# A hybrid encoder block on one core: narrower score and value products, and new due times for a planned order

## The chip, the cores and the metric

The kernel runs on one core of a Trainium2 chip, as one launch. The metric is device time in microseconds (us); it was 699.15 us before the change, the median of three runs (699.06 to 699.29). The engines go by the names of the profile: PE is TensorE (matrix products), PEld is its loading of stationary operands, DVE is VectorE, ACT is ScalarE, POOL is GpSimd, SP is SyncE, which here only issues DMAs.

## The reference

One block over 512 tokens of width 1024, all in float32. Cut to what matters:

```
hn = rms_norm(h, ln_mix)
q1,q2,k1,k2,va, qf,kf,vf,fg, qc,kc,vc = split(hn @ w_in)      # 3590 columns
# three groups of heads, 64 wide: A (4, two score maps each), B (6), C (6)
s  = q @ k.T * scale + bias          # bias: ALiBi / forget gate / relative position
pr = softmax(where(allowed, s, -1e30))    # A: pr1 - lam * pr2
o  = pr @ v                          # A: rms_norm per head behind it
h  = h + concat(o_a, o_b, o_c) @ w_out
h  = h + conv_gated_mlp(rms_norm(h), w_up, conv_w, conv_b, w_down)   # 2816 wide
h  = h + (p @ w_ple_proj) * sigmoid(rms_norm(h) @ w_ple_gate)
```

A query sees keys of its own and earlier chunks of 64 only (B: of its own and earlier positions), so a block of 128 queries needs scores against the key blocks up to its own: 128, 256, 384 and 512 keys for the four query blocks.

## The kernel before, in words

Tokens lie in four blocks of 128. Every weight product is done in float32r (the reduced float32 that PE takes) as three products, high by high, high by low and low by high, so that float32 accuracy is kept; a weight tile is loaded (SP), cast to its high part (ACT, `whi`) and subtracted to its low part (DVE or POOL, `wlo`). One PE instruction multiplies a stationary operand of 128 by 128 with a moving operand of 128 rows by up to 512 columns, into one of eight PSUM banks: `z` (2), `s` (2), `t` (3), `o` (1).

The first 280 us or so hold the input projection (steps in1_0 to in9_3, three products each of a token block, up to 384 columns) with the attention of the heads laid between. For a head the steps are: `qk_cols` (PE transposes of `zn` into a `t` bank, then `q`, `k` and the low part `kl`), `scores`, `prob_cols`, `values`. `softmax_map` does a query block's scores as two products into an `s` bank, `k` and `kl` against `q`; DVE adds the bias and finds the maximum (`e`, `st`), ACT takes exp. Its width is `N = max(L, 256)`: the first query block needs L = 128 columns and computes 256. There are 20 such maps (16 heads, A has two each), and 16 heads in `values`, where four key blocks are accumulated into the `o` bank. Each is a high and a low product (`pth` and `ptl` for key blocks 0 and 1, `ptc` for 2 and 3); key block 3 concerns 128 queries only, but is moved as 256 columns whose first 128 are zeros (`off = min(kb, 2) * P`). The zeros are written once, by two ACT instructions at the start.

Behind that come the output projection, the gated MLP (22 blocks of the 2816 hidden columns, products of 256 and 512 columns) and the per-layer embedding, whose last steps are named gp.

The order of all instructions is set by a planner in the kernel itself (`Plan`). Every operation is recorded under the step's name, `due` gives PE operations a due time from their place in the written order plus a number of that step in the table `SHIFT`, and all other engines get theirs from the PE operation that needs them. `solve` then places the operations one by one on the engines by estimated durations, the earliest due first. `add` finds what an operation depends on from the regions that it reads and writes; only in the gp steps it takes a matmul as writing its whole bank.

Of the kernel before, what the change touches and what calls it, by code (L numbers as in the profile page):

```python
# [11 lines left out]
AF = mybir.ActivationFunctionType  # L12
# [3 lines left out]
P = 128  # L16
# [25 lines left out]
for _i in range(3):  # L42
# [8 lines left out]


SHIFT = {
# [41 lines left out]
}  # L95


# [29 lines left out]
class Plan:  # L127
# [26 lines left out]
    def add(self, eng, name, a, k):  # L154
# [4 lines left out]
        op.ready = 0.0  # L159
        for w, v in sorted(seen, key=lambda x: x[0]):  # L160
            r = self.region(v)
            if k.get("skip_group_check") and w and self.group.startswith("gp"):
                r = (0, P, 0, 4 * S)
            p0, p1, c0, c1 = r
            stand_in = STAND_INS.get(v.tensor.name)
            where = stand_in.place if stand_in and not stand_in.whole else v.tensor.name
            for other, _, _ in self.mem.get(stand_in.place, ()) if stand_in and stand_in.whole else ():
                if other.end is None:
                    op.deps.append(other)
            if where not in self.mem and v.tensor.space != bass.MemoryType.DRAM:  # L170
                op.ready = max(op.ready, self.fresh)
            log = self.mem.setdefault(where, [])
            for other, (q0, q1, d0, d1), t in self.there:
                if other == v.tensor.name and c0 < d1 and d0 < c1:
                    op.ready = max(op.ready, t)
            keep = []
            for rec in log:
                other, w2, (q0, q1, d0, d1) = rec
                hit = p0 < q1 and q0 < p1 and c0 < d1 and d0 < c1
                if hit and (w or w2) and other is not op:  # L180
                    if other.end is None:
                        op.deps.append(other)
                    elif not eng.name == other.eng.name == "pe":
                        op.ready = max(op.ready, other.end)
                if not (w and other is not op and p0 <= q0 and q1 <= p1 and c0 <= d0 and d1 <= c1):
                    keep.append(rec)
            keep.append((op, w, r))
            self.mem[where] = keep
# [137 lines left out]
def kernel(ctx: ExitStack, tc: tile.TileContext, x, xt0, xt, pt_in, small, g_ffn_in, bias_c,  # L326
# [266 lines left out]
    for b in range(2):  # L593
        for i in range(2):
            c = HALF[1 - i]
# [235 lines left out]


    ptc = [ap.tile([P, S], F32R, tag=f"ptc{b}", name=f"ptc{b}") for b in range(2)]
    for b in range(2):
        act.activation(ptc[b][:, 0:P], ident, AF.Copy, scale=0.0)

    def head_bias(kind, hd):

# [15 lines left out]

    def softmax_map(m, hh, qb, bias, rowb, name):
        L = (qb + 1) * P
        N = max(L, 256)
        q, k, kl = m[0][hh], m[1][hh], m[2]
        c = slice(qb * P, L)
        sp = bank("s", f"{name}_s")  # L860
        pe.matmul(sp[:, :N], q[:, c], k[:, :N], start=True, stop=False)
        pe.matmul(sp[:, :N], q[:, c], kl[hh][:, :N], start=False, stop=True)
        e = ap.tile([P, L], F32, tag=f"e{qb}", bufs=2, name=f"{name}_e")
        st = ap.tile([P, 4], F32, tag="st", bufs=12, name=f"{name}_st")
        init = 3.0e38
# [39 lines left out]
    def prob_cols(pr, hh):  # L905
# [20 lines left out]
        act.copy(th[:, P:], pt[:, P:])  # L926
        dve.tensor_tensor(out=tl[:, P:], in0=pt[:, P:], in1=f32(th[:, P:]), op=ALU.subtract)
        tiles.append((th[:, 2 * P :], tl[:, 2 * P :]))
        tiles.append((th[:, : 2 * P], tl[:, : 2 * P]))
        PT[pr, hh] = tiles  # L930
        yield

    def values(pr, hh):
# [5 lines left out]
        base = hh * HD  # L939
        po = bank("o", f"{pr}_{hh}_po")  # L940
        for kb in range(NT):
            off = min(kb, 2) * P
            v = V[pr][:, kb, hh * P : (hh + 1) * P]
            for j in range(2):
                pe.matmul(po[:, off:], v, PT[pr, hh][kb][j], start=kb == 0 and j == 0, stop=kb == 3 and j == 1)
# [1202 lines left out]
```

## Time and profile before

| what | us |
|---|---|
| median of three runs | 699.15 |
| profiled execution, from its first to its last instruction (span) | 697.6 |
| what lies around the span (median less span; the profiled execution's own time is not listed apart from it) | 1.55 |
| PE busy | 687.9 |
| DVE busy | 572.9 |
| ACT busy | 423.5 |
| POOL busy | 310.5 |

[...] A wait shows on PEld first: the load of the stationary operand is what carries the wait. From 20 to 640 us the granted clock of PE was 1.00 of full speed in every stretch.

### The profile page before, as it was taken

What the parts mean: (1) busy time and instruction counts of PE and PEld (TensorE: products, weight loads), DVE (VectorE), ACT (ScalarE), POOL (GpSimd) and SP (SyncE); (2) the same over time, 40 slices, a digit from 0 to 9 for tenths busy, and PEclk for the clock granted to TensorE, in tenths of its full rate; (3) what the DMA queues carried; (4) which work ended last, traced back from release to release, by engine and by line L of the source; (5) the groups of instructions that cost most, each with busy time, mean ns of one, the idle gap of its engine ahead of it and who ended that gap; (6) DMA issues with size and microseconds to landing.
All of it is one profiled execution on the core that took longest, in us unless ns stands there. A gap on an engine that the chain in (4) does not pass through costs nothing.

```text
span 697.6 us, 12855 instructions
## 1 busy us (share of the span) xinstructions
PE 687.9 (99%) x4600; PEld 643.3 (92%) x4600; DVE 572.9 (82%) x1159; ACT 423.5 (61%) x812; POOL 310.5 (45%) x418
## 2 busy tenths in 40 slices
PE   7999999999999999999999999999999999999997
PEld 7999999999999888899988999898998898999997
DVE  6688899888887873888996988789898899777867
ACT  6657676666675672766755544556536676446853
POOL 3677676756764661222231333421622502344561
PEclk9999999999999999999999999999999999999999
DMA  9543354413222152585865338764368654132433
GB/s 310 204 128 92 87 149 129 110 64 92 88 62 72 61 114 98 192 240 127 218 162 145 110 93 224 162 187 129 93 176 224 169 159 128 48 105 67 150 117 122
DMA packets 42989, 94.31 MB, mean 135 GB/s; under 512 B 4871, under 2 KB 9607, under 8 KB 42925
## 3 DMA queue, kind: packets, MB, share of 16 engines
q1 hardware_dynamic: 35868, 79.02, 35.8%
q0 software_dynamic: 6768, 14.16, 11.6%
q8 instruction: 36, 0.59, 0.4%
q10 hardware_dynamic: 288, 0.30, 0.1%
q14 instruction: 29, 0.23, 0.1%
HBM read 85.20 MB, written 4.21 MB: 128 GB/s over the span
## 4 chain that ended last, share of the span: by engine, by line
PE 96%; DVE 1%; POOL 1%; DMA 0%; ACT 0%; issue 0%; POOLq 0%
PE z L360 45%; PE s L360 23%; PE t L360 20%; PE o L360 8%; DMA zn<-in_w_in_dram 0%; DVE xh_again L360 0%; POOL rs L360 0%; POOL e L360 0%; DVE xl_again L360 0%; DVE kl L360 0%; DVE rs L360 0%; ACT xh_again L360 0%; POOL wlo L360 0%; DVE oall L360 0%; ACT sq L360 0%
## 5 line engine op out<-in xcount | busy, mean ns | idle before, releaser
L360 ACT CAST whi<-wraw 128x768 fp32r<-128x768 f32 (+2 forms) x146 | 108.4, 761 | 49.2 <-DMA wraw<-in_w_up_dram 10.6
L360 DVE TENSOR_TENSOR wlo<-wraw,whi 128x768 fp32r<-128x768 f32 (+2 forms) x128 | 112.8, 893 | 18.1 <-ACT whi L360 16.2
L360 PE MATMUL z<-whi,Th 128*128 128x384 f32 (+2 forms) x360 | 120.3, 346 | 4.8 <-ACT whi L360 4.6
L360 PE MATMUL z<-wlo,Th 128*128 128x384 f32 (+2 forms) x360 | 119.6, 342 | 0.0
L360 PE MATMUL z<-whi,Tl 128*128 128x384 f32 (+2 forms) x360 | 119.3, 341 | 0.0
L360 PEld LDWEIGHTS z<-whi,Th 128*128 128x128 f32 x360 | 67.8, 190 | 8.4 <-ACT whi L360 4.9
L360 PEld LDWEIGHTS z<-whi,Tl 128*128 128x128 f32 x360 | 67.8, 189 | 2.9
L360 PEld LDWEIGHTS z<-wlo,Th 128*128 128x128 f32 x360 | 68.1, 190 | 2.3
L360 POOL TENSOR_TENSOR wraw<-wraw,wraw 128x768 f32<-128x768 f32 (+2 forms) x21 | 28.1, 1343 | 82.7 <-DVE pin L360 41.0
L360 ACT ACTIVATE e<-e,st 128x128 f32<-128x128 f32 (+3 forms) x80 | 44.6, 559 | 16.6 <-DVE st L360 16.3
L360 PE MATMUL z<-Th,whi 128*128 128x256 f32 (+1 forms) x152 | 51.8, 341 | 0.0
L360 PE MATMUL z<-Tl,whi 128*128 128x256 f32 (+1 forms) x152 | 51.6, 340 | 0.0
L360 PE MATMUL z<-Th,wlo 128*128 128x256 f32 (+1 forms) x152 | 51.5, 340 | 0.0
L360 PE MATMUL s<-Tl,whi 128*128 128x256 f32 (+1 forms) x152 | 51.5, 340 | 0.0
L360 PE MATMUL s<-Th,wlo 128*128 128x256 f32 (+1 forms) x152 | 51.3, 340 | 0.0
L360 PE MATMUL s<-Th,whi 128*128 128x256 f32 (+1 forms) x152 | 51.1, 341 | 0.0
L360 POOL TENSOR_TENSOR rs<-rs,nhalf 128x4 f32<-128x4 f32 x40 | 43.2, 1090 | 4.9 <-DVE rs L360 1.4
L360 DVE CUSTOM_DVE_ANT_0 e<-s,bias 128x128 f32<-128x128 f32 (+3 forms) x74 | 33.9, 471 | 5.4 <-PE s L360 2.8
L360 POOL TENSOR_SCALAR e<-e,st 128x256 f32<-128x256 f32 (+3 forms) x48 | 29.1, 641 | 10.3 <-DVE st L360 8.3
L360 POOL DMA_DIRECT2D wraw<-in_w_up_dram x21 | 18.9, 902 | 31.4 <-DMA wraw<-in_w_up_dram 21.4
L360 PE MATMUL t<-whi,al 128*128 128x256 f32 x116 | 32.2, 282 | 0.0
L360 PE MATMUL t<-wlo,ah 128*128 128x256 f32 x116 | 32.1, 281 | 0.0
(342 smaller groups left out, 2286.6 us busy)
## 6 DMA issues: line engine op xcount, KB each, us to landing
wraw<-in_w_up_dram SPq DMA_DIRECT2D x41, 384.0 KB, 4.5
wraw<-in_w_in_dram SPq DMA_DIRECT2D x28, 384.0 KB, 3.6
wraw<-in_w_down_dram SPq DMA_DIRECT2D x17, 384.0 KB, 3.2
wlo_again<-in_w_up_dram SPq DMA_DIRECT2D x12, 384.0 KB, 4.3
whi_again<-in_w_up_dram SPq DMA_DIRECT2D x11, 384.0 KB, 4.5
wraw<-in_w_out_dram SPq DMA_DIRECT2D x16, 256.0 KB, 2.8
wraw<-in_w_up_dram SPq DMA_DIRECT2D x16, 256.0 KB, 3.9
wlo<-wraw POOLq DMA_DIRECT2D x7, 384.0 KB, 4.8
```

What stands on the lines that cost most here:

```text
L360: ins = getattr(self.eng, op)(*a, **k)
```

## The change

The scores of the first query block are computed 128 columns wide, the values of the last key block are moved 128 columns wide, and the two instructions that wrote the zeros are gone. In the planner, every PE instruction is taken as writing its whole bank. Of the numbers in `SHIFT` all but six are new, 20 steps that had none have one now, and one has lost it; of that table two lines stand here.

```diff
 SHIFT = {
-    "in1_1": 0.4, "in1_2": -4.5, "A0a": 0.1, "in1_3": -3.6, "in2_0": -0.9, "in2_1": 1, "A0b": 23.2, "in2_2": -4.2,
...
+    "in1_1": 0.6, "in1_2": -16.6, "A0a": 11.4, "in1_3": 2.9, "in2_0": 13.5, "in2_1": 16, "A0b": 24, "in2_2": 0.5,
...
@@ Plan.add
             r = self.region(v)
-            if k.get("skip_group_check") and w and self.group.startswith("gp"):
+            if w and eng.name == "pe":
                 r = (0, P, 0, 4 * S)
...
     ptc = [ap.tile([P, S], F32R, tag=f"ptc{b}", name=f"ptc{b}") for b in range(2)]
-    for b in range(2):
-        act.activation(ptc[b][:, 0:P], ident, AF.Copy, scale=0.0)
...
@@ softmax_map
         L = (qb + 1) * P
-        N = max(L, 256)
...
-        pe.matmul(sp[:, :N], q[:, c], k[:, :N], start=True, stop=False)
-        pe.matmul(sp[:, :N], q[:, c], kl[hh][:, :N], start=False, stop=True)
+        pe.matmul(sp[:, :L], q[:, c], k[:, :L], start=True, stop=False)
+        pe.matmul(sp[:, :L], q[:, c], kl[hh][:, :L], start=False, stop=True)
...
@@ prob_cols
-        tiles.append((th[:, : 2 * P], tl[:, : 2 * P]))
+        tiles.append((th[:, P : 2 * P], tl[:, P : 2 * P]))
...
@@ values
-            off = min(kb, 2) * P
+            off = kb * P
```

The program has 4,598 PE instructions before and after. 72 of them, which were 256 columns wide, are 128 now: 40 scores (20 maps, `k` and `kl`) and 32 values (16 heads, high and low). Apart from the two ACT instructions no other operation is added or removed, but nearly all of the program past the first 66 PE instructions stands in another order. Three places show it. In the rows, `s_130` and `s_131` are the two banks of scores, `t_146`, `t_149`, `t_150` those of transposes, `z_128` and `z_129` those of the projection, `o_148` the bank of values; a product reads moving operand, stationary operand; L360 and L363 are the same line of the helper that issues everything.

Place 1 is PE at the values of a head of A0, with the projection and transposes that stand between them. Before:

```order
L360 MATMUL z_129<-wlo_118,Th_64 128x256
L360 MATMUL o_148<-ptc_0_138,V_142 128x256
L360 MATMUL z_129<-whi_117,Tl_66 128x256
L360 MATMUL o_148<-ptc_0_137,V_142 128x256
L360 MATMUL z_129<-whi_120,Th_64 128x256
L360 MATMUL o_148<-ptc_0_138,V_142 128x256
L360 MATMUL z_129<-wlo_121,Th_64 128x256
```

And now, at the other head of A0:

```order
L363 MATMUL t_150<-ident,zn_91 128x128
L363 MATMUL o_148<-ptc_0_138,V_142 128x256
L363 MATMUL t_150<-ident,zn_91 128x128
L363 MATMUL o_148<-ptc_0_137,V_142 128x128
L363 MATMUL t_150<-ident,zn_91 128x128
L363 MATMUL o_148<-ptc_0_138,V_142 128x128
L363 MATMUL t_146<-ident,zn_91 128x128
L363 MATMUL z_129<-wlo_111,Th_64 128x384
```

The last two value products are 128 wide now, and here each is followed by a transpose; of the 72 narrow products 16 are followed by a transpose, 2 by another narrow one and 54 by a wider float32r product.

Place 2 is PE at the second score map of A0's first head. Before:

```order
L360 MATMUL t_149<-ident,bias_87 128x128 x3
L360 MATMUL s_130<-k_159,q_157 128x256
L360 MATMUL s_130<-kl_0_102,q_157 128x256
L360 MATMUL z_129<-whi_108,Th_64 128x384
L360 MATMUL z_129<-wlo_109,Th_64 128x384
L360 MATMUL z_129<-whi_108,Tl_66 128x384
L360 MATMUL z_129<-whi_108,Th_64 128x384
L360 MATMUL z_129<-wlo_109,Th_64 128x384
L360 MATMUL s_130<-k_159,q_157 128x384
L360 MATMUL s_130<-kl_0_102,q_157 128x384
```

And now:

```order
L363 MATMUL s_130<-k_159,q_157 128x128
L363 MATMUL z_128<-whi_114,Tl_67 128x384
L363 MATMUL s_130<-kl_0_102,q_157 128x128
L363 MATMUL t_149<-ident,bias_87 128x128 x4
L363 MATMUL s_130<-k_159,q_157 128x256
L363 MATMUL s_130<-kl_0_102,q_157 128x256
L363 MATMUL s_130<-k_159,q_157 128x384
L363 MATMUL s_130<-kl_0_102,q_157 128x384
L363 MATMUL z_129<-whi_108,Th_64 128x384
```

Before, five projection products stood between the scores of the second and of the third query block in bank `s_130`; now the third block's scores follow the second's in the same bank with nothing between.

Place 3 is PE at the first value product of A0's second head, which needs the cast `pth_181` of a bank of transposes. Before:

```order
L360 MATMUL t_149<-ident,e_0_95 128x128
L360 MATMUL z_129<-wlo_127,Th_65 128x256
L360 MATMUL t_149<-ident,e_0_95 128x128
L360 MATMUL z_129<-whi_126,Tl_67 128x256
L360 MATMUL z_129<-whi_126,Th_65 128x256
L360 MATMUL z_129<-wlo_127,Th_65 128x256
L360 MATMUL z_129<-whi_126,Tl_67 128x256
L360 MATMUL o_148<-pth_181,V_142 128x512
L360 MATMUL t_146<-ident,zn_91 128x128 x3
```

And now:

```order
L363 MATMUL t_146<-ident,e_0_95 128x128
L363 MATMUL z_128<-whi_114,Th_65 128x384
L363 MATMUL z_128<-wlo_115,Th_65 128x384
L363 MATMUL z_128<-whi_114,Tl_67 128x384
L363 MATMUL z_129<-whi_108,Th_64 128x384
L363 MATMUL z_129<-wlo_109,Th_64 128x384
L363 MATMUL z_129<-whi_108,Tl_66 128x384
L363 MATMUL o_148<-pth_181,V_142 128x512
L363 MATMUL t_149<-ident,zn_92 128x128
```

The value product stood four products of 256 columns behind the head's last transpose; now it stands six products of 384 columns behind it.

## Rows read from the trace of the kernel before

**Rows 1.** The page's parts 1 (busy time) and 4 (chain that ended last).
```profile
PE 687.9 (99%) x4600; PEld 643.3 (92%) x4600; DVE 572.9 (82%) x1159; ACT 423.5 (61%) x812; POOL 310.5 (45%) x418
...
PE 96%; DVE 1%; POOL 1%; DMA 0%; ACT 0%; issue 0%; POOLq 0%
```

**Rows 2.** Timeline, first 5 us: start, duration, engine, what, [idle before <-releaser].
```profile
2.95 0.51 ACT L360 ACTIVATE ptc<-ident 128x128 fp32r<-128x128 f32 x2
...
4.06 0.51 ACT L360 CAST whi<-zn 128x384 fp32r<-128x384 f32 x1 [0.60 <-DMA zn<-in_w_in_dram]
...
4.62 1.01 PE L360 MATMUL z<-whi,Th 128*128 128x384 f32 x2 [4.62 <-ACT whi L360]
```

**Rows 3.** Waits of PEld: who for whom, us in total, times, longest.
```profile
PEld z L360 <- ACT whi L360: 4.9, 2, 4.6
PEld s L360 <- DVE st L360: 0.9, 3, 0.4
PEld t L360 <- DVE zn L360: 0.6, 2, 0.4
...
PEld t L360 <- ACT pth L360: 0.4, 1, 0.4
...
PEld o L360 <- DVE ptl L360: 0.2, 1, 0.2
```

**Rows 4.** Groups by form: what, shape, count | busy, mean ns.
```profile
L360 PE MATMUL o<-ptc,V 128*128 128x256 f32 x64 | 17.0, 296 | 0.0
...
L360 PE MATMUL s<-k,q 128*128 128x256 f32 x40 | 11.4, 309 | 0.1
...
L360 PE MATMUL s<-kl,q 128*128 128x256 f32 x40 | 10.8, 298 | 0.0
```

**Rows 5.** Timeline of PE in two dense stretches, 512 and 256 columns.
```profile
109.63 0.39 PE L360 MATMUL s<-k,q 128*128 128x512 f32 x1
109.86 0.39 PE L360 MATMUL s<-kl,q 128*128 128x512 f32 x1
...
687.77 0.28 PE L360 MATMUL t<-whi,al 128*128 128x256 f32 x1
...
688.60 0.28 PE L360 MATMUL z<-whi,ah 128*128 128x256 f32 x1
```

**Rows 6.** Timeline of PE and PEld around a wait at 42.6 us.
```profile
42.65 0.19 PEld L360 LDWEIGHTS s<-k,q 128*128 128x128 f32 x1 [0.39 <-POOL k L360]
42.65 0.39 PE L360 MATMUL s<-k,q 128*128 128x256 f32 x1
...
42.76 0.19 PEld L360 LDWEIGHTS z<-wlo,Th 128*128 128x128 f32 x1
```

**Rows 7.** Transposes: the tile `e` (ns min/median/max), and two places of the timeline.
```profile
L360 PEld LDWEIGHTS t<-ident,e x160: 138/140/145, 56.3 to 265.7; 128*128 128x128 f32 x160
L360 PE MATMUL t<-ident,e x160: 270/272/328, 56.5 to 266.0; 128*128 128x128 f32 x160
...
116.19 0.93 PE L360 MATMUL t<-ident,e 128*128 128x128 f32 x7
...
132.34 0.20 PEld L360 LDWEIGHTS t<-ident,zn 128*128 128x128 f32 x2 [0.42 <-DVE zn L360]
```

**Rows 8.** The one float32 product: a place of the timeline, and its group.
```profile
88.18 1.02 PE L360 MATMUL o<-otmp,oall 128*128 128x512 f32 x2
...
L360 PE MATMUL o<-otmp,oall 128*128 128x512 f32 x4 | 2.0, 591 | 0.0
```

**Rows 9.** The wait of place 3, and DVE's reading of 256 columns of scores.
```profile
76.36 0.28 PE L360 MATMUL z<-whi,Tl 128*128 128x256 f32 x1
...
76.66 0.19 PEld L360 LDWEIGHTS o<-pth,V 128*128 128x128 f32 x1 [0.22 <-ACT pth L360]
76.66 0.50 PE L360 MATMUL o<-pth,V 128*128 128x512 f32 x1
...
L360 DVE CUSTOM_DVE_ANT_0 e<-s,bias 128x256 f32<-128x256 f32 x20 | 8.3, 420 | 0.7 <-PE s L360 0.4
```

83 rows, old and new, of the table SHIFT are left out of this document.

## The prediction

> **What bounds the kernel now.** I read the page first. PE is busy for 687.9 of 697.6 us, the next engine, DVE, for 572.9, and the chain that ended last is PE for 96% [rows 1]: the kernel is bound by what PE issues, and an engine off PE matters only where PE waits for it. The waits are therefore the second view. They stand on PEld: 17 rows, which add up to 10.6 us; 4.6 of that is the start, until the first cast weight arrives [rows 2, 3]. The remaining 6.0 us, single waits of 0.2 to 0.4 us for DVE, ACT and POOL, are the most that any new order of the program could win past the start; it is an upper end, because a load also counts as idle while the product before it still moves. The third view is the timeline of dense stretches, for the price of one product: two of 512 columns start 0.23 us apart, and seven distances of 256-column products take 0.83 us, 0.118 each [rows 5]. The mean durations of the groups that the change touches, 0.296 to 0.309 us [rows 4], are no price, since neighbours overlap.
>
> **The narrow products.** 72 products go from 256 to 128 columns: half of the 80 scores and half of the 64 values that rows 4 count at 256. Scaled by columns they would fall from 0.118 to about 0.06 us: the slope is (0.23 - 0.118)/256, so 128 columns are worth 0.056 us. But each product also needs its own stationary operand, and one place shows what that load takes when nothing covers it. At 42.65 us PE had waited for POOL, so the load of a score product lies bare: the product lasts 0.39 us instead of 0.28, and the next load starts 0.11 us after the first, just when the product begins to move [rows 5, 6]. So a float32r load takes 0.11 us, and the load for the following product begins only when the present one starts to move. Behind a 256-column product that load is covered (0.118 against 0.11). Behind a 128-column one it is not: the next float32r product can't start before 0.11 us. For 54 + 2 narrow products, which are followed by float32r, the saving is 0.118 - 0.11, some 0.008 us: 56 x 0.008 = 0.45 us.
>
> A transpose's load is shorter: two loads of 0.14 us take 0.20 together when they lie bare, so the second began 0.06 after the first [rows 7]. The 16 narrow products followed by a transpose, as at place 1, thus cost their own 0.06 us: 16 x 0.058 = 0.93 us. Together 1.4 us. The stage is PE's (it waits for little else), so I count it whole.
>
> For the ends: no float32r product under 256 columns stands in the trace. From below, all 72 at the column price win 72 x 0.058 = 4.2 us. From above, the nearest row of another rate is the plain float32 product, two records of 0.591 us that span 1.02, so 0.43 us apart and 0.86 for 512 columns [rows 8]; at that rate 128 columns take 0.215, and 72 x 0.097 = 7.0 us are lost. I take the load-bound price because it is nearest to what the rows show on the same kind of instruction; transposes, also 128 columns wide, are (0.93 - 0.27)/6 = 0.11 us apart [rows 7], which is the same sum.
>
> The bare load of rows 6 took 0.11 us, and that sets the sum above. [...]
>
> **The zeros.** The two ACT instructions lie at 2.95 to 3.46 us, and ACT then idles 0.60 us for the first weights' DMA [rows 2]. Removing them wins nothing; with that cover gone they would have cost 0.5 us.
>
> **The new order.** It can't add PE work (the count is unchanged), so it acts through waits alone. I weigh the places where they differ. At place 3 PE lost 0.3 us at 76.66: the value product started 0.30 us behind the one before it instead of 0.118, and lasted 0.50 instead of 0.39 since its load lay bare [rows 5, 9]. Added up with the spacings above, it stood 0.93 us of PE work behind the last transpose of the bank whose cast it needs, and now stands 1.16 us behind it. Over all heads, seven value products stood 1.05 us or less behind that transpose; now one does. PEld's waits for these casts and their low parts are four of its 17 rows, 0.4, 0.3, 0.2 and 0.2 us, of which rows 3 hold the first and the last; I count 0.8 of these 1.1 us as won. Late next is the low part from DVE, which stood behind the cast anyway. At place 2 the opposite happens: the third block's scores need the bank that DVE still has to read. The second block's last product ends 0.28 us after its start, DVE's read of 256 columns takes 0.42 [rows 9], and then the load lies bare for 0.11: 0.81 us instead of 0.118, so some 0.7 us are lost, and all of PE's queue behind it, the projection first, stands for so long. Two more score pairs (0.44 and 0.55 us behind the bank's last use, by the same count) may lose 0.1 to 0.2 us each. What the waits for `zn` and `st` become (1.5 us together, rows 3) can't be read from the order, since they hang on DVE's queue. That leaves gains and losses of about 1 us each that are known and, in the rest, up to some 3 us to be won, and hardly as much to be lost, as none of it is new work. The loads that SP and POOL issue move with their steps; past the start no row of PEld's waits names a DMA, so I count them at nothing, and a weight that came late would show as a wait for its cast `whi`, which is 0.3 us at most now. I take -0.5 us for the order, between -2.5 and +1.4. Taking whole banks as written changes no instruction; it only makes the planner keep products from a bank that another engine reads, and its effect is in this term.
>
> **Sum.** -1.4 - 0.5 = -1.9 us: a span of 695.7 instead of 697.6, and with the 1.55 us that lie between span and median, 697.2 us instead of 699.15 (-0.27%).
>
> **The rivals.** First, the loads hide after all and the narrow products run at column price: for it speaks that PEld is not busy all the time, against it rows 6 and the fixed order of one load ahead. -4.2 - 0.5 gives 694.4 us. [...] Second, the slower side: below 256 columns a float32r product falls back to the rate of plain float32. For it speaks that no such product was in the program and that a slower rate exists on this PE [rows 8]; against it that transposes of 128 columns, which are float32 too, take only 0.11 us. It decides from about 0.125 us per narrow product on (0.118, and the order's 0.5 us over 72); at full price it is +7.0 - 0.5, 705.6 us. Third, the narrow products go as forecast, but place 2 is typical of the new order and its waits give the gain back: +1.4 from waits makes 699.2 us. Fourth, that the change doesn't do what it says can be left out: the order of the changed program shows the 72 narrow products.
>
> **How the numbers follow.** Forecast 0.60, column price 0.07, float32's rate 0.13, waits give it back 0.20. About 0.2%, 1.4 us, is what a measurement of this kernel can tell from no change: faster means under 697.75, slower over 700.55. The forecast's own range is 695.2 to 699.2, by the order's ends; two thirds of it lie under 697.75. Faster: 0.60 x 0.68 + 0.07 = 0.48. Slower: 0.13 and a quarter of the third rival, 0.18. Same: the rest, 0.34. The range from 694.6 to 700.4 takes in the forecast, nearly all of the third rival and a little of the first, and leaves out the second.
>
> **What would show it.** In the profile of the changed kernel, a narrow score product followed by a projection product: the latter should start (or end) about 0.11 us later than a column-bound product would, with its load beginning at the narrow one's start; followed by a transpose, 0.06. At 0.06 throughout, the first rival holds, at 0.2 the second. At place 2 a wait of PEld for DVE's `st` of about 0.7 us, at place 3 none for `pth`. The sum of PEld's waits should stay at 5 to 6 us past the start; at 8 the third rival is true. Wrong would be the whole account if PE's idle time moved by several us at places where neither a narrow product nor a bank's reuse stands.

## The result, and the profile after

The changed kernel takes 702.35 us (median of four runs, 701.81 to 703.15) against 699.11 us of the kernel before on the same chip: a ratio of 1.0046, 95% interval 1.0031 to 1.006. It is slower by 0.46%. The forecast was 697.2 us, and its range ended at 700.4.

The page of the profiled execution (702.13 us, span 700.4), its parts 1 and 4, to be read against [rows 1]:

```profile
PE 686.6 (98%) x4600; PEld 642.4 (92%) x4600; DVE 574.8 (82%) x1159; ACT 425.9 (61%) x810; POOL 315.2 (45%) x418
...
PE 89%; POOL 3%; DMA 3%; DVE 2%; issue 1%; ACT 1%; POOLq 0%; ACTq 0%; DVEq 0%
```

PE is busy 1.3 us less than before and the span is 2.8 us longer. The chain, 96% PE before, now runs for 11% through other engines; POOL, 1% before, has 3%. So PE's work did not grow: PE stands still for longer. POOL's busy time has grown from 310.5 to 315.2 us with the same 418 instructions. That points at POOL.

The waits of PEld, all eleven rows (who waits for whom, us in total, times, longest), against [rows 3]:

```profile
PEld z L363 <- ACT whi L363: 4.6, 1, 4.6
PEld s L363 <- POOL k L363: 3.6, 4, 1.3
PEld s L363 <- DVE st L363: 1.6, 3, 0.7
PEld o L363 <- ACT otmp L363: 1.3, 1, 1.3
PEld z L363 <- issue: 1.0, 4, 0.2
PEld z L363 <- DVE conv L363: 0.9, 2, 0.6
PEld z L363 <- DVE Tl L363: 0.5, 1, 0.5
PEld o L363 <- issue: 0.5, 1, 0.5
PEld t L363 <- ACT whi L363: 0.3, 1, 0.3
PEld s L363 <- DVE wlo L363: 0.2, 1, 0.2
PEld t L363 <- DVE wlo L363: 0.2, 1, 0.2
```

Past the start they add up to 10.1 us instead of 6.0. The many small waits for `zn`, `pth` and `ptl` are gone; in their place stand four waits for `k` from POOL (3.6 us), three for `st` (1.6) and one for `otmp` (1.3). The same by another count, each PE instruction's distance end to end from the one before it less what such an instruction usually takes (0.118, 0.175 or 0.233 us for 256, 384 or 512 columns, 0.109 for a transpose, 0.43 for a float32 product), added up from 14 us on: PE lost 5.2 us before and 9.8 after.

The narrow products, one place of PE's timeline (start, duration) and PEld's beside it:

```profile
57.39 0.34 PE L363 MATMUL z<-whi,Th 128*128 128x384 f32 x1
57.56 0.22 PE L363 MATMUL s<-k,q 128*128 128x128 f32 x1
57.62 0.39 PE L363 MATMUL z<-wlo,Th 128*128 128x384 f32 x1
57.85 0.22 PE L363 MATMUL s<-kl,q 128*128 128x128 f32 x1
...
57.56 0.19 PEld L363 LDWEIGHTS z<-wlo,Th 128*128 128x128 f32 x1
57.67 0.19 PEld L363 LDWEIGHTS s<-kl,q 128*128 128x128 f32 x1
```

The product behind the narrow one starts 0.06 us after it, but lasts 0.39 instead of 0.34: its load began only at 57.56, with the narrow product, and took until 57.67, as the bare load of [rows 6] did. From the end of the first row to the end of the third are 0.28 us, of which 0.175 are the 384 columns; so the narrow product costs 0.11. Over all 54 such places a narrow product ends 0.06 behind the one before it, and its follower of 256, 384 or 512 columns ends 0.171, 0.227 or 0.285 behind the narrow product: together about 0.113 and the follower's own price. Before a transpose, narrow product and transpose together take 0.06 + 0.134 = 0.194, of which 0.109 are the transpose's: 0.085 for the narrow one.

Place 2, PE and DVE's reading of the second block's scores:

```profile
53.52 0.28 PE L363 MATMUL s<-kl,q 128*128 128x256 f32 x1
54.32 0.45 PE L363 MATMUL s<-k,q 128*128 128x384 f32 x1 [0.52 <-DVE st L363]
...
53.84 0.42 DVE L363 CUSTOM_DVE_ANT_0 e<-s,bias 128x256 f32<-128x256 f32 x1
```

The third block's scores start 0.80 us behind the second's, as forecast (0.81). Place 3's wait is gone.

Now the first trace of the cause in single instructions. POOL's copies of the low half of `q` and `k` (the helper `move`, 64x512), of which a head's scores need the last. The group of the tile `k`, ns min/median/max, after and then before:

```profile
L363 POOL TENSOR_SCALAR k<-k x30: 613/618/2027, 38.9 to 258.2; 64x512 fp32r<-64x512 f32 x30
```

```profile
L360 POOL TENSOR_SCALAR k<-k x30: 612/617/782, 38.2 to 247.0; 64x512 fp32r<-64x512 f32 x30
```

The same copy takes 0.61 us, or up to 2.03. Of all 60 copies ten take over 0.7 us (0.87 to 2.03), three before. Two places of the timeline of after, POOL and DVE, show what stands beside the long ones:

```profile
50.65 1.58 POOL L363 TENSOR_SCALAR k<-k 64x512 fp32r<-64x512 f32 x1
...
51.09 0.66 DVE L363 TENSOR_TENSOR wlo<-wraw,whi 128x512 fp32r<-128x512 f32 x1
...
52.28 0.33 PE L363 MATMUL s<-k,q 128*128 128x128 f32 x1 [0.58 <-POOL k L363]
...
156.79 1.87 POOL L363 TENSOR_TENSOR wlo<-wraw,whi 128x768 fp32r<-128x768 f32 x1 [0.23 <-ACT whi L363]
...
156.86 2.61 DVE L363 TENSOR_TENSOR wlo<-wraw,whi 128x768 fp32r<-128x768 f32 x1
...
160.56 0.69 DVE L363 TENSOR_TENSOR oall<-o,otmp 64x512 f32<-64x512 f32 x1
...
161.29 0.63 ACT L363 ACTIVATE otmp<-oall 128x512 f32<-128x512 f32 x1 [1.30 <-DVE oall L363]
...
161.97 1.13 PE L363 MATMUL o<-otmp,oall 128*128 128x512 f32 x2 [0.94 <-ACT otmp L363]
```

At 50.65 us a copy stands beside DVE's subtraction of two SBUF tiles and ends 0.48 us behind it; PE waits for that copy. All ten long copies stand beside such a subtraction for at least a part of their time (one of them, at 209.64 us, only for its last 0.19). At 156.86 it is the other way round: DVE's subtraction, 0.95 us by its median, takes 2.61 beside a subtraction of POOL's. DVE's queue is late by 1.7 us, with it `oall`, ACT's `otmp` and at last PE. The theory from here on: an instruction on POOL and a subtraction of two SBUF tiles on DVE that run side by side hinder each other, so that one of the two ends late. The rivals: narrow products that cost more than thought, waits that belong to the new order itself, or due times that only fit other rules.

### The profile page after: what moved, and what is told of

Read it like the earlier page. It is cut to its first block, busy times and chain, and to the rows that moved or that the text cites. A ratio compares the mean times of both kernels' runs of the same rounds, so it can differ in the third digit from the quotient of the medians.

```text
span 700.4 us, 12856 instructions
## 1 busy us (share of the span) xinstructions
PE 686.6 (98%) x4600; PEld 642.4 (92%) x4600; DVE 574.8 (82%) x1159; ACT 425.9 (61%) x810; POOL 315.2 (45%) x418
## 4 chain that ended last, share of the span: by engine, by line
PE 89%; POOL 3%; DMA 3%; DVE 2%; issue 1%; ACT 1%; POOLq 0%; ACTq 0%; DVEq 0%
PE z L363 41%; PE s L363 21%; PE t L363 19%; PE o L363 8%; DMA wraw<-in_w_up_dram 2%; POOL k L363 2%; POOL q L363 1%; DMA zn<-in_w_in_dram 0%; POOL wraw L363 0%; DVE conv L363 0%; POOL wlo_again L363 0%; ACT whi L363 0%; DVE wlo L363 0%; ACT otmp L363 0%; DVE xl_again L363 0%
## 5 line engine op out<-in xcount | busy, mean ns | idle before, releaser
L363 ACT CAST whi<-wraw 128x768 fp32r<-128x768 f32 (+2 forms) x146 | 109.4, 762 | 51.9 <-PE z L363 16.5
L363 DVE TENSOR_TENSOR wlo<-wraw,whi 128x768 fp32r<-128x768 f32 (+2 forms) x128 | 113.8, 901 | 17.3 <-ACT whi L363 16.3
L363 PE MATMUL z<-whi,Th 128*128 128x384 f32 (+2 forms) x360 | 123.1, 348 | 4.6 <-ACT whi L363 4.6
L363 PE MATMUL z<-whi,Tl 128*128 128x384 f32 (+2 forms) x360 | 122.9, 347 | 0.1
L363 PE MATMUL z<-wlo,Th 128*128 128x384 f32 (+2 forms) x360 | 122.5, 346 | 0.0
L363 PEld LDWEIGHTS z<-whi,Th 128*128 128x128 f32 x360 | 67.9, 189 | 7.9 <-ACT whi L363 4.6
L363 PEld LDWEIGHTS z<-whi,Tl 128*128 128x128 f32 x360 | 67.8, 189 | 3.8 <-DVE Tl L363 0.5
L363 PEld LDWEIGHTS z<-wlo,Th 128*128 128x128 f32 x360 | 67.8, 189 | 3.2
L363 POOL TENSOR_TENSOR wraw<-wraw,wraw 128x768 f32<-128x768 f32 (+2 forms) x21 | 29.7, 1416 | 66.9 <-DVE pin L363 25.9
L363 ACT ACTIVATE e<-e,st 128x128 f32<-128x128 f32 (+3 forms) x80 | 44.7, 560 | 23.7 <-DVE st L363 23.0
L363 PE MATMUL s<-Tl,whi 128*128 128x512 f32 (+1 forms) x152 | 51.9, 341 | 0.0
L363 PE MATMUL s<-Th,whi 128*128 128x256 f32 (+1 forms) x152 | 51.7, 342 | 0.0
L363 PE MATMUL s<-Th,wlo 128*128 128x256 f32 (+1 forms) x152 | 51.7, 341 | 0.0
L363 PE MATMUL z<-Th,wlo 128*128 128x256 f32 (+1 forms) x152 | 51.4, 340 | 0.0
L363 PE MATMUL z<-Tl,whi 128*128 128x256 f32 (+1 forms) x152 | 51.3, 340 | 0.0
L363 PE MATMUL z<-Th,whi 128*128 128x256 f32 (+1 forms) x152 | 51.2, 341 | 0.0
L363 POOL TENSOR_TENSOR rs<-rs,nhalf 128x4 f32<-128x4 f32 x40 | 42.3, 1060 | 5.4 <-DVE rs L363 2.9
L363 DVE CUSTOM_DVE_ANT_0 e<-s,bias 128x128 f32<-128x128 f32 (+3 forms) x74 | 34.0, 471 | 11.7 <-PE s L363 9.1
L363 POOL TENSOR_SCALAR e<-e,st 128x512 f32<-128x512 f32 (+3 forms) x48 | 28.4, 602 | 24.4 <-DVE st L363 19.4
L363 PE MATMUL t<-wlo,ah 128*128 128x256 f32 x116 | 32.7, 282 | 0.0
L363 PE MATMUL t<-whi,al 128*128 128x256 f32 x116 | 32.7, 282 | 0.0
L363 PE MATMUL t<-whi,ah 128*128 128x256 f32 x116 | 32.4, 282 | 0.0
```

The source lines that it names most:

```text
L363: ins = getattr(self.eng, op)(*a, **k)
```

## The experiments

**The two halves of the change apart.** First the 72 products at 128 columns in exactly the order of before, on every engine:

```diff
-        pe.matmul(sp[:, :N], q[:, c], k[:, :N], start=True, stop=False)
+        pe.matmul(sp[:, :N], q[:, c], k[:, :N], start=True, stop=False, swap=(sp[:, :L], q[:, c], k[:, :L]))
```

(`swap` holds the operands that are issued; the planner still sees the first ones. The values likewise; the zeros are still written.)

> The order of every engine is that of the kernel before, row for row; only the 72 products are 128 instead of 256 columns wide (the zeros are still written). Theory A (the loss comes from the new order; a narrow product saves little, because the next load isn't covered): in the trace after the change a narrow product and the float32r product behind it together end 0.005 us earlier than with 256 columns, with a transpose behind it 0.033 us earlier; here 61 have a product and 11 a transpose behind them, so -0.7 us: 698.4. Theory B (the narrow products themselves are what is slow, at float32's rate or by waits that they bring): +3 us or more. Theory C (column price, as the first rival had it): -4 us.

698.34 us (697.96 to 698.97), ratio 0.9992, interval 0.9983 to 1.0001: the narrow products win about 0.7 us, at the edge of what can be told.

Then the order of after with 256 columns, by the same device (the zeros are written at the start):

```diff
-        pe.matmul(sp[:, :L], q[:, c], k[:, :L], start=True, stop=False)
+        N = max(L, 256)
+        pe.matmul(sp[:, :L], q[:, c], k[:, :L], start=True, stop=False, swap=(sp[:, :N], q[:, c], k[:, :N]))
```

> The order of every engine is that of the changed kernel, row for row; only the 72 products are 256 columns wide again (and the zeros are written at the start, beside the first DMAs). Theory A: the loss stays, and the narrow products' 0.8 us are given back, in part into PE's waits: 702.4 to 703.2. Theory B: the loss goes, about 699.

702.6 us (702.28 to 703.01), ratio 1.0052 (1.004 to 1.0065). The loss is all in the order. PE's four waits for `k` stand in front of narrow score products in the changed kernel; with 256 columns the row is the same, so they do not come from the width:

```profile
PEld s L366 <- POOL k L366: 3.6, 4, 1.3
```

**The stretched copies on ACT.** After's order; the ten copies over 0.7 us are done by ACT at the same place of the program:

```diff
+                if len(MOVES) - 1 in ON_ACT:      # ten of the 60 copies
+                    return act.now("copy", a[:2], {}, pinned)
```

> The changed kernel in its own order, but the ten copies of q and k parts that POOL did in more than 0.7 us instead of 0.61 are done by ACT, at the same place of the order. Theory A1 (POOL's copies are stretched where DVE subtracts two SBUF operands beside them, and PE waits for the last copy of k: 0.8, 1.2, 0.4 and 0.6 us): PE's four waits for POOL go, -2.5 to -3 us, 699.5 us. Theory A2 (those copies stand too late in the order whoever does them): less than 1 us of change, 702.

699.39 us (698.68 to 701.35), ratio 1.0008 (1.0 to 1.0017): 3.0 us of the loss come back, and PE no longer waits for POOL's `k`. The copies that are left on POOL:

```profile
L370 POOL TENSOR_SCALAR k<-k x23: 611/617/625, 39.5 to 255.8; 64x512 fp32r<-64x512 f32 x23
...
L370 ACT CAST k<-k x7: 617/620/622, 51.5 to 256.7; 64x512 fp32r<-64x512 f32 x7
...
L370 POOL TENSOR_SCALAR q<-ql x19: 612/616/2007, 37.4 to 257.2; 64x512 fp32r<-64x512 f32 x19
```

The copies of `k` show no stretch any more. Four copies of `q` do (1.05 to 2.01 us): they now stand on POOL beside the DVE instructions where others stood. No row of PEld's waits names them: by this trace PE does not wait for them, and nothing shows that they cost time.

**The second collision.** On top of that, DVE's subtraction at 156.9 us goes six places back in DVE's queue, behind `oall` (with the refill of its raw tile, which SP issues):

```diff
+MOVED = [(1693, 1724), (1704, 1726)]   # place in the planned order, the place before which it is put
...
+            for a, b in MOVED:
+                order.remove(was[a])
+                order.insert(order.index(was[b]), was[a])
```

> The changed kernel's order with the ten stretched copies on ACT, and one more edit: DVE's subtraction wlo at 156.9 us, which stood beside POOL's subtraction and took 2.61 instead of 0.95 us, moves six places back in DVE's queue. Theory P (the wait of 1.2 us for otmp at 162 us comes from that stretch, since DVE's oall stands behind it): the wait goes, 699.4 - 1.2 = 698.2 us, between 697.9 and 698.6. Theory R (the wait belongs to the order: ACT and DVE come to otmp late anyway): 699.2 to 699.6 us, and PE still waits about 1.2 us at 162 us.

698.11 us (697.53 to 699.25, one outlier of 1125 us left aside), ratio 0.9988 (0.9978 to 0.9997). The timeline of DVE and PE:

```profile
158.36 0.56 DVE L382 TENSOR_TENSOR ptc<-t,ptc 128x384 fp32r<-128x384 f32 x1 [0.90 <-ACT ptc L382]
...
159.90 0.69 DVE L382 TENSOR_TENSOR oall<-o,otmp 64x512 f32<-64x512 f32 x1 [0.18 <-ACT otmp L382]
160.71 1.81 DVE L382 TENSOR_TENSOR wlo<-wraw,whi 128x768 fp32r<-128x768 f32 x2
...
161.38 1.07 PE L382 MATMUL o<-otmp,oall 128*128 128x512 f32 x2
```

PE no longer waits for `otmp` at this place, and the moved subtraction with the one behind it takes 1.81 us for both. The move takes the whole subtraction out of the queue ahead of `oall`, not the stretch alone. But DVE now stands idle for 0.90 us ahead of `ptc`, which waits for ACT: an unstretched subtraction of 0.95 us would have fitted there, so it is the stretch that made `oall` late. With these stretches out of PE's way the new order, 698.11 us, stands where the old one with the same narrow products does, 698.34. The two edits together bring back 702.35 - 698.11 = 4.2 us, which is all of the order's loss (702.35 - 698.34 = 4.0) within what can be told.

**The collision by itself.** Stages added behind the last step of the kernel before, each begun by an ACT instruction that writes what both engines read:

```diff
+    def copy(i):      # POOL, 64x512
+        pool.tensor_scalar(c[:64, i * 512 : i * 512 + 512], f32(a[:64, :512]), 1.0, 1.0, ALU.mult, ALU.mult)
+    def two(eng, t, i=0):      # two SBUF operands, 128x768
+        eng.tensor_tensor(out=t[:, i * 768 : i * 768 + 768], in0=f32(a[:, :768]), in1=f32(b[:, :768]), op=ALU.subtract)
+    def bank_read():      # one from PSUM, one from SBUF, 128x512
+        dve.tensor_tensor(out=d[:, :512], in0=bk, in1=f32(a[:, :512]), op=ALU.subtract)
```

> The program of before, with a row of small stages added behind its last step (so its time is some 40 us longer and not compared): in each, ACT writes an operand in SBUF and then POOL and DVE start on it together. Theory P (POOL and DVE hinder each other where both take two streams from SBUF): POOL's copy of 64x512 takes 0.61 us alone and beside DVE's subtraction that reads PSUM, but is stretched to 1.2 to 1.6 us beside DVE's subtraction of two SBUF operands (0.94 us) and to 2 us or more beside two such subtractions; DVE's subtraction, started after POOL's subtraction of 768 columns (1.87 us alone), takes 2.0 to 2.6 us instead of 0.94. Theory Q (the stretched copies come from something else of the changed program, as the many semaphores or the load of SBUF by all engines): the copy takes 0.6 to 0.7 us in every stage, and DVE's subtraction 0.94.

The timeline of POOL, then of DVE:

```profile
695.22 0.62 POOL L360 TENSOR_SCALAR Tl<-Th 64x512 fp32r<-64x512 f32 x1 [13.33 <-ACT Th L360]
...
702.12 1.80 POOL L360 TENSOR_TENSOR Tl<-Th,Th 128x768 fp32r<-128x768 f32 x1 [4.71 <-issue]
...
707.61 1.38 POOL L360 TENSOR_SCALAR Tl<-Th 64x512 fp32r<-64x512 f32 x1 [0.95 <-ACT Th L360]
...
712.26 0.61 POOL L360 TENSOR_SCALAR Tl<-Th 64x512 fp32r<-64x512 f32 x1 [0.94 <-ACT Th L360]
...
723.49 0.61 POOL L360 TENSOR_SCALAR Tl<-Th 64x512 fp32r<-64x512 f32 x1 [1.81 <-ACT Th L360]
...
726.78 1.80 POOL L360 TENSOR_TENSOR Tl<-Th,Th 128x768 fp32r<-128x768 f32 x1 [1.03 <-ACT Th L360]
...
734.00 1.80 POOL L360 TENSOR_TENSOR Tl<-Th,Th 128x768 fp32r<-128x768 f32 x1 [1.81 <-ACT Th L360]
```

```profile
698.30 0.96 DVE L360 TENSOR_TENSOR Tl<-Th,Th 128x768 fp32r<-128x768 f32 x1 [4.08 <-ACT Th L360]
...
707.55 0.96 DVE L360 TENSOR_TENSOR Tl<-Th,Th 128x768 fp32r<-128x768 f32 x1 [6.44 <-ACT Th L360]
...
712.42 1.26 DVE L360 TENSOR_TENSOR Tl<-Th,Th 128x768 fp32r<-128x768 f32 x1
...
723.44 0.69 DVE L360 TENSOR_TENSOR Tl<-t,Th 128x512 fp32r<-128x512 f32 x1 [0.95 <-ACT Th L360]
...
726.93 2.46 DVE L360 TENSOR_TENSOR Tl<-Th,Th 128x768 fp32r<-128x768 f32 x1
...
733.96 0.69 DVE L360 TENSOR_TENSOR Tl<-t,Th 128x512 fp32r<-128x512 f32 x1 [0.95 <-ACT Th L360]
```

Every stage stands twice; the second time gives the same durations within 0.01 us. Alone the copy takes 0.62, POOL's subtraction 1.80 and DVE's 0.96 us. At 707.6 DVE begins 0.06 us ahead: its subtraction keeps 0.96, the copy takes 1.38 and ends 0.48 behind it. At 712.3 a small DVE instruction stands in front of DVE's subtraction, so the copy begins 0.16 ahead: it keeps 0.61, and DVE's takes 1.26. At 726.9, behind POOL's subtraction, DVE's takes 2.46. At 723.5 and 734.0, where DVE takes one operand from PSUM, neither POOL's copy nor its subtraction nor DVE's (0.69) is slower. One figure was missed: beside two subtractions of DVE in a row the copy took 1.38 as well, not 2 us or more; it goes between the two, which together take 2.24 instead of 1.92.

So these rows show who hinders whom: a subtraction of two SBUF tiles on DVE and a copy or a subtraction on POOL. The one that goes first keeps its time (0.96 us for DVE's subtraction, 0.61 for the copy, 1.80 for POOL's subtraction), and the other ends 0.48 us (the copy) or about 0.81 us (DVE's subtraction) behind it. What it is in the two engines or in SBUF that makes the other late, the rows do not show.

**Due times and the rules that they were found for.** Four plans mix the old and the new. First, the changed kernel with the table of before:

```diff
 SHIFT = {
-    "in1_1": 0.6, "in1_2": -16.6, "A0a": 11.4, "in1_3": 2.9, "in2_0": 13.5, "in2_1": 16, "A0b": 24, "in2_2": 0.5,
+    "in1_1": 0.4, "in1_2": -4.5, "A0a": 0.1, "in1_3": -3.6, "in2_0": -0.9, "in2_1": 1, "A0b": 23.2, "in2_2": -4.2,
...
```

> Narrow products and whole banks as in the changed kernel, planned with the due times of the kernel before; the planner makes a third order of it. Theory A in the form that the new due times are to blame: as fast as before or 0.7 us faster, 698.4 to 699.5. If instead any order that the planner makes anew, with due times that were found for other rules, has such waits: 700 to 703, like the changed kernel.

728.46 us (726.97 to 728.73), ratio 1.0418 (1.0404 to 1.0432): far above both ranges. The old table does not rescue the changed kernel. Second, before with the rule on whole banks alone:

```diff
-            if k.get("skip_group_check") and w and self.group.startswith("gp"):
+            if w and eng.name == "pe":
```

> The kernel before with one rule of the planner changed, whole banks taken as written; its old due times and 256 columns stay. Theory S (due times are worth something only under the rules for which they were found: any change of a rule spoils the plan): 705 to 730 us, with PE's waits 8 us or more above those of before. Theory W (the 728 us of old due times with both new rules came from the narrow widths in the plan): 698.5 to 700.5 us.

725.48 us (724.62 to 729.09), ratio 1.0385 (1.0362 to 1.0407), in the range of theory S; PEld's waits past the start add up to 29.2 us. Third, before with the narrow products in the plan, old due times and old rule:

```diff
-        N = max(L, 256)
...
-            off = min(kb, 2) * P
+            off = kb * P
```

> The kernel before with the 72 products 128 wide in the plan itself, so that the planner prices them anew and sets another order; its old due times and its old rule for banks stay. Theory S (due times are worth something only for the rules and prices for which they were found; whole banks alone with the old ones made 725.5 us): 703 to 725 us, with PE's waits several us above those of before. Rival W (the rule on banks alone spoils the old due times): 697.8 to 700.5 us, as the same widths in the unchanged order made 698.3.

710.23 us (709.96 to 711.77), ratio 1.0169 (1.0152 to 1.0186), again in the range of theory S. Fourth, after with 256 columns and the zeros, planned anew with the new due times:

```diff
+        N = max(L, 256)
...
-            off = kb * P
+            off = min(kb, 2) * P
```

> The changed kernel's due times and its rule for banks, with 256 columns and the zeros as before, planned anew: the counterpart of the changed order with 256 columns, which kept the order and made 702.6 us. Theory S (due times fit only the prices for which they were found): 706 to 725 us. Rival W (only the rule on banks moves much): 701.5 to 704 us.

727.02 us (725.46 to 728.81), ratio 1.0403 (1.0382 to 1.0425), even above the range given. So "new due times" are not an addition to the other two edits that could be weighed by itself: each of these four mixtures of table and rules loses 11 to 29 us. That other mixtures would too is not shown. One place where it goes, in the second, is this stretch from 140 us on (busy us and instructions of each engine, granted clock, DMA share, GB/s):

```profile
140.00:160.00 20.00, 19.89 (x122) 18.14 (x121) 17.98 (x75) 14.11 (x38) 11.63 (x20) 1.00 0.13 40
160.00:170.00 10.00, 7.31 (x36) 6.08 (x35) 6.66 (x13) 5.05 (x10) 4.71 (x6) 0.83 0.60 160
170.00:175.00 5.00, 1.77 (x5) 1.77 (x6) 4.90 (x11) 3.17 (x10) 4.84 (x5) 0.66 0.16 43
175.00:180.00 5.00, 5.00 (x23) 5.00 (x23) 2.48 (x4) 1.16 (x3) 3.85 (x7) 0.66 0.34 116
180.00:200.00 20.00, 19.27 (x117) 18.22 (x117) 15.91 (x56) 11.52 (x28) 10.37 (x15) 1.00 0.19 60
```

PE is idle for 5.9 us between 160 and 175 (it waits for `ptl` and `wlo` from DVE). The granted clock falls within this stretch, from 1.00 to 0.83 on the mean from 160 to 170 us and to 0.66 from 170 to 180. From 175 to 180 us PE is busy throughout and gets through 23 instructions, 0.22 us for each; from 180 to 200 us, with the clock at 1.00 again, it is 19.27 us for 117, 0.165 for each (widths are mixed in both). So by these counts time goes twice here: into the waits, and into slower products behind them. That the waits are what lowers the clock is not shown.

**A better order.** The experiments point to the old order with narrow products. In it PE still loses 4.6 us past the start by the count above, most of it in waits of 0.1 to 0.4 us. Twelve PE instructions, each ready by the trace, are taken forward into nine of these waits, with the same `MOVED` as above:

```diff
+MOVED = [(1148, 1146), (1496, 1415), (1499, 1415), (1502, 1415), (1483, 1481), (1545, 1544), (1754, 1753), (1775, 1753), (1898, 1893), (1896, 1895), (2026, 2016), (2534, 2533)]
```

> The order of before with the 72 products 128 wide (698.3 us), and twelve PE instructions taken forward into nine of the waits that PE still has there: each stands a few places before, was ready by the trace, and does not depend on what it passes. Theory A (the order acts through a few waits of 0.1 to 0.4 us, each of which a ready instruction can fill): the filled waits add up to 1.7 us, and with some 0.4 us that turns up behind them 698.3 - 1.3 = 697.0 us, between 696.6 and 697.5. Rival F (PE's waits past the start are set by the chain of the other engines, so a filled wait comes back at the next place): 698.1 to 698.5 us.

696.98 us (696.45 to 697.49), ratio 0.9968 (0.9955 to 0.998): faster than before by 0.32%, than after by 5.4 us, and the fastest of all. PEld's wait for `zn` at 131 us, 0.4 us in [rows 3], is 0.2 now, those for `e` at 162 and `pth` at 235 us are gone; of what was filled, 1.7 us, 1.4 stayed won, since a few others grew, as that for `oall` at 186 us from 0.13 to 0.28. Theory A holds and rival F does not: most of what was filled stayed filled. The nine were filled in one run, so what each is worth by itself is not shown.

## Why the prediction was wrong

*PE is the bound, and an order acts through waits alone.* Right: PE's busy time fell, and the span grew by waits.

*The order, "-0.5 us for the order, between -2.5 and +1.4", of which up to 3 us to be won and "hardly as much to be lost, as none of it is new work".* This is the step that failed, and it turned the sign. The runs put the order at +4.0 us: 702.35 with the new one and 698.34 with the old, both with the narrow products. Instructions are not of fixed length here: a copy on POOL or a subtraction on DVE grows by 0.3 to 1.7 us when the order lays the two beside each other, so a new order can be new work in effect. The prediction counted what PE waits for and distances on PE and at places on DVE; it did not compare which POOL instruction now stands beside which of DVE. Four waits for `k` (3.1 us of PE's time) and one for `otmp` (1.2) come from it, and taking them away brings the time to 698.1. The rest of the order, with the gains and losses named in the prediction, comes out at nothing that can be told: 698.11 with the new order, 698.34 with the old.

*The narrow products, -1.4 us.* The mechanism was right (the next load begins with the narrow product, both at 57.56 us, and is what counts), the size was too large. With a float32r product behind it the narrow one costs 0.113 against 0.118 us, so 0.005 is saved and not 0.008: 56 x 0.005 = 0.3 instead of 0.45 us. Before a transpose it costs 0.085, not 0.06: 16 x 0.033 = 0.5 instead of 0.93. The term that was mis-sized is "cost their own 0.06 us": it took the transpose's shorter load (0.14 us by [rows 7], where a product's is 0.19) to be hidden altogether behind the 0.06 us. Together 0.8 us by the trace, about 0.7 in the run with the old order, whose interval (0.9983 to 1.0001) just takes in no change. Neither column price nor float32's rate was seen anywhere, so the first two rivals fall.

*The zeros, nothing.* PE's first product begins at 4.60 us without them and at 4.62 with them, so nothing shows that they cost or covered anything. They were not measured alone.

*Places 2 and 3.* Right: 0.80 us between the scores forecast at 0.81, and the wait for `pth` is gone.

*The rivals and the signs.* The third rival, waits that give the gain back, is true by the sign that was named for it (8 us of PEld's waits past the start; they are 10.1), but its price was 1.4 us against 4 and its place was wrong: what place 2 shows is not what most of the loss is made of. The last sign named came closer: PE's idle time moved by several us at places that no bank's reuse explains and, as the order with 256 columns shows, no narrow product either. What should have been a rival of its own was in the code: the planner's `held` keeps POOL and such DVE instructions apart, but only in its own clock; in the first plan no wait is emitted for it, so that nothing keeps them apart on the chip where its times differ from the plan's.

## What to carry to other kernels

When an order changes, compare not only what stands before what on the bounding engine, but which instructions of POOL and DVE now run side by side: an unchanged instruction whose maximum is three times its median, as 2.03 us is to 0.62 here (view by tile), is the first thing to look for. Then ask whether the bounding engine waits for it; a stretched copy for which PE did not wait cost nothing that showed. A table of due times is worth something only with the rules and prices that it stands with here; the four mixtures cost 11 to 29 us, where the narrow products win about 0.7. Change the emitted operands in a fixed order first, to learn what an edit is worth, and then fill single waits by hand.

## What was not expected of the hardware

- In the added stages POOL and DVE hinder each other where DVE reads two operands from SBUF: 0.61 becomes 1.38 us for a copy, 0.96 becomes 2.46 for a subtraction behind POOL's. With one operand from PSUM nothing happens (0.69 and 0.61).
- Open: at 50.65 us of the changed kernel the copy is recorded 0.44 us ahead of DVE's subtraction and yet is the one that waits, while in the added stages a lead of 0.16 us was enough to go first. How exact POOL's recorded starts are was not measured, and what decides in a copy right behind another was not tried. Open too is the copy at 209.64 us (0.94 us): for most of its time the DVE instruction beside it was one with an operand in PSUM (`oall`, 209.78 to 210.45), and the next subtraction of two SBUF tiles begins only at 210.38.
- At the start products of 384 columns stand 0.32 us apart and then 0.175, in the profiled execution of before fifteen of them and of after eight. PE had been at work since 4.6 us. The trace's record of the granted clock begins only there, with 1.00, at 10.0 us in before and at 7.7 in after; for the time ahead of it there is no record, and a view that prints 1.00 for it has measured nothing. The difference is worth about 1 us in favour of after in these two executions. The first 66 PE instructions are the same in both, so the order on PE is not what sets it; how much it varies between executions of one kernel was not measured.
